# Weight rings without padding, `y` and the mix at byte 64 of a 2048-byte line, and a longer block-wise end in a two-layer fp32 encoder

## The chip, the core and the metric

One core of a Trainium2 chip runs the whole program in one launch. The metric is the time of one execution in microseconds on the device; the kernel before took 2162.01 us (median of 3 runs, 2161.94 to 2162.14). TensorE (PE) multiplies; each of its multiplications is a weight load (PEld, the stationary operand, 128 columns) and a matmul (the moving operand). VectorE (DVE), ScalarE (ACT) and GpSimd (POOL) do the elementwise work, SyncE (SP) issues the transfers.

## What is computed

An encoder of two residual layers on 256 tokens of width 2048, all in fp32. Layer 0 has chunked and differential attention, layer 1 a sparse attention with an indexer and a shared latent. Cut to what matters here:

```python
for layer in range(DEPTH):                       # DEPTH = 2
    h = rmsnorm(x, attn_norm[layer])
    if layer % 2 == 0:
        p = h @ even_w_in[e]                     # 2048 x 6144: q, k, v of both head groups
        mix = jnp.concatenate([oa, ob], axis=-1) @ even_w_out[e]      # 2048 x 2048
    else:
        p = h @ odd_w_in[o]                      # q, latent, index parts
        mix = oc.reshape(b, s, C_Q_W) @ odd_w_out[o]                  # 2048 x 2048
    x = x + mix
    h = rmsnorm(x, ffn_norm[layer])
    x = x + (jax.nn.silu(h @ w_gate[layer]) * (h @ w_up[layer])) @ w_down[layer]   # 2048 x 5632, 5632 x 2048
return rmsnorm(x, final_norm)
```

## The kernel before

**Split numbers.** Every fp32 operand is held as a rounded high part and the rest: `xs` (normalized input), `y` (FFN hidden) and `mix` hold `[tile, 2, 256]` with the high part at index 0 and the low part at index 1, so that the two are 1024 bytes apart and one tile takes 2048 bytes of a partition. A weight piece (128 x 1024 fp32, 512 KB) lands in `wl`, a ring of 5; ACT rounds it to `wh` (line 145), DVE writes the rest to `wo` (line 146). `wh` and `wo` are rings of 3, so the next piece's `wh` can be written once PE is done with the piece three before it. `load_w` does this, `next_w` keeps three pieces ahead.

**Two forms of product.** `gemm_t` has the weights stationary and the activations moving. For each piece it makes 4 groups (`n`) of 4 matmuls, by `products`: two of 512 columns with `wh` (high and low part of an `xs` tile together), then two of 256 columns with `wo` (high part alone). This is the gate and up projection (352 pieces), q and k (64), the odd layer's q (32) and its index part (8): 456 pieces with 1824 groups, whose results are named `acc`. `gemm_n` has the activations stationary and the weights moving, 512 columns at a time. For each piece, two token blocks `b`, two tiles `j` and three matmuls by `mm3`: (`y` high, `wh`), (`y` high, `wo`), (`y` low, `wh`), so 12 matmuls. This is `w_down` (176 pieces), the two output projections (32 each) and the four v projections (32): 272 pieces, whose results are named `nat`. All of them go through `mm`, so that they are recorded at one line, 181.

**The places.** Inside a partition each `wh` and `wo` buffer is padded on both sides by `OFF` = 16 floats, so the ring's step is 4224 bytes and not 4096. The v pieces and `w_uv` are written 64 bytes into the buffer (`moving`, `UVO`), all others at its start. `spacer` tiles of `SP0`, `SP1` and `SPY` floats set where `mix` (layer 0, layer 1) and `y` begin. In the built program the places, as bytes modulo 2048, are:

| | place 0 | place 1 | place 2 |
|---|---|---|---|
| `wh` | 1600 | 1728 | 1856 |
| `wo` | 1984 | 64 | 192 |

`xs` is at 128, `y` at 1088 in both layers, `mix` at 1088 in layer 0 and at 448 in layer 1. The loads go round the ring, so that pieces follow each other in places 1, 0, 2, 1 and so on as seen by PE.

**The end.** The last of the four column groups of `w_down` in layer 1 is made with `last=2`: 20 pieces are worked off with both token blocks alternating, and the last two pieces first for block 0 and then for block 1. After each block `finish_block` adds the residual (line 312, DVE), squares (line 307, ACT), forms 1/rms (lines 271, 255, 257), scales four column parts (lines 674, 676, 678) and writes them out (line 679).

Each engine's instructions stand in the order of the code; nothing reorders them.

Of the kernel before, what the change touches and what calls it, by code (L numbers as in the profile page):

```python
# [25 lines left out]
FT = DFF // P  # L26
# [13 lines left out]
def encoder_kernel(  # L40
# [41 lines left out]
    def bank(shape, name):  # L82
        return psum.tile(shape, F32, name=name, tag="ps")


    OFF = 16
    SP0, SP1, SPY = 16, 16, 96
    UKO, UVO = 0, OFF
    OUT0 = [4, 5, 6, 7, 0, 1, 2, 3]
    QUADS = (2, 3, 0, 1)  # L90

# [10 lines left out]
    def moving(pieces):  # L102
        return ((src, OFF) for src in pieces)

# [25 lines left out]
    def load_w(cuts=1, between=None):  # L130
# [7 lines left out]
        wl = wpool.tile([P, width], F32, name="wl", tag="wl", bufs=5)  # L138
        wh, wo = (wpool.tile([P, width + 2 * OFF], F32R, name=n, tag=n, bufs=3)[:, off:off + width] for n in ("wh", "wo"))
        for i in range(cuts):  # L140
# [8 lines left out]
    def next_w():  # L149
        while len(ahead) < 3:  # L150
            n = len(ahead)
            load_w()
            if len(ahead) == n:
                break
        return ahead.popleft()
# [4 lines left out]
    def pump(n=1):  # L160
        for _ in range(n):
            while steps:
                try:
                    next(steps[0])
                    break
                except StopIteration:
                    steps.popleft()
# [15 lines left out]
    def mm3(out, a, b, start, stop):  # L183
        (ah, al), (bh, bl) = a, b
        mm(out, ah, bh, start, False)
        mm(out, ah, bl, False, False)
        mm(out, al, bh, False, stop)
# [26 lines left out]
    def gemm_n(lhs, nk, order=None, last=0, done=None):  # L214

        banks = [bank([P, 512], f"nat{i}") for i in range(2)]
        order = list(range(nk // 2)) if order is None else order

        def block_products(b, i, w):
            wh, wo = w  # L220
            for j in range(2):
                h, l = lhs(2 * order[i] + j)
                t = slice(b * P, (b + 1) * P)
                c = slice(j * 512, (j + 1) * 512)
                mm3(banks[b], (h[:, t], l[:, t]), (wh[:, c], wo[:, c]),
                    i == 0 and j == 0, i == len(order) - 1 and j == 1)

        for i in range(len(order) - last):
            w = next_w()
            for b in range(2):  # L230
                block_products(b, i, w)
                pump()
        if last:
            ws = [next_w() for _ in range(last)]
            for b in range(2):
                for i, w in enumerate(ws):
                    block_products(b, len(order) - last + i, w)
                done(b, banks[b])
        return banks

    def pairs(act):
        return lambda kt: (act[:, kt, 0, :], act[:, kt, 1, :])
# [59 lines left out]
    def new_sums():  # L302
        return {"sums": small.tile([P, 2, 4], F32, name="sums", tag="sums", bufs=2)}
# [5 lines left out]
    def add_block(bk, b, g, st):  # L309

        c = xn[:, b, 512 * g:512 * g + 512]
        nc.vector.tensor_tensor(out=c, in0=bk, in1=c, op=ALU.add)
        add_squares(st, b, g)
# [15 lines left out]
    def add_residual(banks, g, gi, st):  # L329
        for b in range(2):  # L330
            add_block(banks[b], b, g, st)
        steps.append(transpose_steps(g, gi))
# [284 lines left out]
    def ffn(st):  # L617

        with tc.tile_pool(name="ffn", bufs=1) as fp:
            fp.tile([P, SPY], F32, name="spacer")  # L620
            y = fp.tile([P, FT, 2, S], F32R, name="y")
            for g in range(FT // 4):
                gb = gemm_t(xs, KT)
                if g == 0:
                    drain()
                ga = fp.tile([P, 4, S], F32, name="ga", tag="ga", bufs=1)
                for n in range(4):
                    a = ga[:, n, :]
                    combined(a, gb[n])
                    nc.vector.tensor_tensor(out=a, in0=a, in1=st["rr"], op=ALU.mult)  # L630
                    th = fp.tile([P, S], F32, name="th", tag="th", bufs=3)
                    nc.scalar.activation(th, a, AF.Tanh, scale=0.5)  # L632
                    nc.vector.scalar_tensor_tensor(out=a, in0=th, scalar=1.0, in1=a, op0=ALU.add, op1=ALU.mult)  # L633
                    nc.gpsimd.tensor_tensor(out=a, in0=a, in1=st["rs"], op=ALU.mult)  # L634
                ub = gemm_t(xs, KT)
                for n in range(4):
                    t = 4 * g + n
                    a = ga[:, n, :]
                    u = fp.tile([P, S], F32, name="up", tag="up", bufs=2)
                    combined(u, ub[n])  # L640
                    nc.vector.tensor_tensor(out=a, in0=a, in1=u, op=ALU.mult)
                    split((y[:, t, 0, :], y[:, t, 1, :]), a)
            yield y, fp

    def ffn_layer(st, gi, last):
        out = new_sums()
        body = ffn(st)
        y, fp = next(body)
        if last:
            gf = fp.tile([P, D], F32, name="gf", tag="ga", bufs=1)  # L650
            nc.sync.dma_start(out=gf, in_=bass.AP(tensor=gfin.tensor, offset=gfin.offset, ap=[[0, P], [1, D]]))
        for g in range(4):
            fin = last and g == 3
            banks = gemm_n(pairs(y), FT, last=2 if fin else 0, done=partial(finish_block, out, gf) if fin else None)
            if not last:
                add_residual(banks, g, gi, out)
            elif not fin:
                for b in range(2):
                    add_block(banks[b], b, g, out)
                    c = slice(512 * g, 512 * g + 512)  # L660
                    nc.gpsimd.tensor_tensor(out=xn[:, b, c], in0=xn[:, b, c], in1=gf[:, c], op=ALU.mult)
        for _ in body:
            pass
        return out
# [15 lines left out]

    steps.append(norm_steps(st, "n1", 0.5))
    st = ffn_layer(st, 2, False)


# [9 lines left out]
    banks = [bank([P, 2, S], f"x{n}") for n in range(3)]  # L694
# [135 lines left out]

    steps.append(norm_steps(st, "n3", 0.5))
    ffn_layer(st, 4, True)


# [61 lines left out]
```

## Time and profile before

| | |
|---|---|
| median of 3 runs | 2162.01 us |
| the profiled execution | 2161.7 us, of which its span 2159.9 us |
| PE busy | 2148.4 us, 99% of the span |
| DVE, ACT, POOL busy | 60%, 49%, 8% |
| chain that ended last | PE 98% (`acc` 59%, `nat` 35%) |
| granted TensorE clock | 0.999 of 2.4 GHz |

Matmuls are pipelined: the duration of one in the record is longer than the time from its start to the next one's start. How fast PE goes is read from the distances of starts, or from a stretch's length and its count.

### The profile page before, as it was taken

How to read it: one execution, taken by the hardware profiler on the slowest of the kernel's cores; microseconds unless marked ns; L12 is line 12 of the kernel's file. 1: busy time of each engine (PE TensorE's matmuls, PEld its weight loads, DVE VectorE, ACT ScalarE, POOL GpSimd, SP SyncE). 2: the span in 40 equal slices, each digit the busy share in tenths (PEclk: the TensorE clock that was granted, in tenths of full speed). 3: DMA queues.
4: the chain of work that ended last, by engine and by line, in shares of the span. 5: the costliest groups of instructions: out<-in, count | busy, mean ns of one | idle time of the engine just before them, and what ended most of it. 6: DMA issues, size and time to landing. Idle time of an engine off the chain costs nothing.

```text
span 2159.9 us, 29908 instructions
## 1 busy us (share of the span) xinstructions
PE 2148.4 (99%) x11380; PEld 1836.1 (85%) x11380; DVE 1299.2 (60%) x1882; ACT 1065.6 (49%) x1603; POOL 178.6 (8%) x194
## 2 busy tenths in 40 slices
PE   9999999999999999999999999999999999999998
PEld 8888888888888888888888888888888888888886
DVE  6665555666666666544446977556666666654443
ACT  6554554545454454444435566445454454543443
POOL 0111000000000000000001241000000000000000
PEclk9999999999999999999999999999999999999999
DMA  9565556555555665555656554555555555566564
GB/s 319 174 178 167 175 167 184 184 186 186 189 188 189 187 188 191 186 185 187 193 168 214 166 156 151 182 186 186 189 189 188 187 189 190 186 207 193 187 193 138
DMA packets 114975, 401.95 MB, mean 186 GB/s; under 512 B 12618, under 2 KB 16526, under 8 KB 114702
## 3 DMA queue, kind: packets, MB, share of 16 engines
q1 hardware_dynamic: 114686, 399.90, 58.7%
q8 instruction: 89, 1.46, 0.3%
q14 instruction: 56, 0.46, 0.1%
q10 hardware_dynamic: 144, 0.13, 0.0%
HBM read 397.84 MB, written 2.14 MB: 185 GB/s over the span
## 4 chain that ended last, share of the span: by engine, by line
PE 98%; DMA 1%; DVE 0%; ACT 0%; issue 0%; SPq 0%; ACTq 0%; POOLq 0%; POOL 0%
PE acc L181 59%; PE nat L181 35%; PE x L181 1%; PE uk L181 1%; DMA xt<-in_xT 1%; PE xT L323 0%; PE is L181 0%; PE c3o L181 0%; PE a0o L181 0%; PE a1o L181 0%; PE c2o L181 0%; PE c0o L181 0%; PE c1o L181 0%; DVE wo L146 0%; PE b31o L181 0%
## 5 line engine op out<-in xcount | busy, mean ns | idle before, releaser
L146 DVE TENSOR_TENSOR wo<-wl,wh 128x1024 fp32r<-128x1024 f32 (+2 forms) x747 | 925.9, 1240 | 805.2 <-ACT wh L145 797.3
L145 ACT ACTIVATE wh<-wl 128x1024 fp32r<-128x1024 f32 (+2 forms) x747 | 786.9, 1054 | 910.1 <-PE acc L181 491.9
L181 PE MATMUL acc<-xs,wh 128*128 128x512 f32 x3648 | 1147.7, 396 | 0.5 <-ACT wh L145 0.5
L181 PEld LDWEIGHTS acc<-xs,wo 128*128 128x128 f32 x3648 | 685.6, 188 | 160.2 <-DVE wo L146 1.6
L181 PE MATMUL acc<-xs,wo 128*128 128x256 f32 x3648 | 731.1, 281 | 0.6 <-DVE wo L146 0.5
L181 PEld LDWEIGHTS acc<-xs,wh 128*128 128x128 f32 x3648 | 560.3, 188 | 3.2 <-ACT wh L145 0.8
L181 PE MATMUL nat<-wh,y 128*128 128x512 f32 x1408 | 441.6, 394 | 0.0
L181 PEld LDWEIGHTS nat<-wh,y 128*128 128x128 f32 x1408 | 264.2, 188 | 61.4
L181 PE MATMUL nat<-wo,y 128*128 128x512 f32 x704 | 276.4, 393 | 0.0
L181 PE MATMUL nat<-wh,mix 128*128 128x512 f32 x512 | 166.7, 397 | 0.0
L181 PEld LDWEIGHTS nat<-wo,y 128*128 128x128 f32 x704 | 132.3, 188 | 29.8
L337 ACT ACTIVATE u<-acc 128x256 f32<-128x256 f32 x228 | 86.3, 379 | 61.4 <-PE acc L181 32.3
L181 PEld LDWEIGHTS nat<-wh,mix 128*128 128x128 f32 x512 | 96.1, 188 | 21.1
L181 PE MATMUL nat<-wo,mix 128*128 128x512 f32 x256 | 100.4, 392 | 0.0
L181 PE MATMUL nat<-wh,xs 128*128 128x512 f32 x256 | 83.2, 393 | 0.0
L634 POOL TENSOR_TENSOR ga<-ga,n1rs 128x256 f32<-128x256 f32 x44 | 37.7, 867 | 440.3 <-DVE ga L633 417.2
L634 POOL TENSOR_TENSOR ga<-ga,n3rs 128x256 f32<-128x256 f32 x44 | 36.6, 843 | 441.4 <-DVE ga L633 418.3
L181 PEld LDWEIGHTS nat<-wh,xs 128*128 128x128 f32 x256 | 48.1, 188 | 10.0
L181 PEld LDWEIGHTS nat<-wo,mix 128*128 128x128 f32 x256 | 48.2, 188 | 9.7
L181 PE MATMUL nat<-wo,xs 128*128 128x512 f32 x128 | 50.0, 391 | 0.0
L298 ACT ACTIVATE xs<-xT,gc 128x256 fp32r<-128x256 f32 x48 | 22.4, 467 | 31.0 <-DVE xs L299 31.0
L632 ACT ACTIVATE th<-ga 128x256 f32<-128x256 f32 x88 | 33.8, 410 | 5.8 <-DVE ga L630 5.7
(804 smaller groups left out, 1056.3 us busy)
## 6 DMA issues: line engine op xcount, KB each, us to landing
wl<-in_w_gate SPq DMA_DIRECT2D x176, 512.0 KB, 3.8
wl<-in_w_up SPq DMA_DIRECT2D x176, 512.0 KB, 3.6
wl<-in_w_down SPq DMA_DIRECT2D x176, 512.0 KB, 3.6
wl<-in_w_ein SPq DMA_DIRECT2D x93, 512.0 KB, 3.6
wl<-in_w_eout SPq DMA_DIRECT2D x32, 512.0 KB, 3.6
wl<-in_w_oq SPq DMA_DIRECT2D x32, 512.0 KB, 3.6
wl<-in_w_oout SPq DMA_DIRECT2D x32, 512.0 KB, 3.5
wl<-in_w_oi SPq DMA_DIRECT2D x8, 512.0 KB, 4.2
```

The costliest lines, as they stand in the source:

```text
L145: latest["act"] = nc.scalar.activation(wh[:, c], wl[:, c], AF.Copy)
L146: nc.vector.tensor_tensor(out=wo[:, c], in0=wl[:, c], in1=wh[:, c].bitcast(F32), op=ALU.subtract)
L181: nc.tensor.matmul(out, a, b, start=start, stop=stop, skip_group_check=True)
L298: nc.scalar.activation(xs[:, t, 0, :], src, AF.Copy, scale=g)
L337: nc.scalar.activation(u[:m], b[:m, 0, :], AF.Copy)
L632: nc.scalar.activation(th, a, AF.Tanh, scale=0.5)
L634: nc.gpsimd.tensor_tensor(out=a, in0=a, in1=st["rs"], op=ALU.mult)
```

## The change

`OFF` becomes 0, so the rings of `wh` and `wo` step by 4096 bytes and no piece is written 64 bytes in. The spacers move `y` and `mix`. The last three pieces (before: two) are worked off block by block.

```diff
-    OFF = 16
-    SP0, SP1, SPY = 16, 16, 96
-    UKO, UVO = 0, OFF
+    OFF = 0
+    SP0, SP1, SPY = 464, 112, 32
+    UKO, UVO = 0, 0
@@
-            banks = gemm_n(pairs(y), FT, last=2 if fin else 0, done=partial(finish_block, out, gf) if fin else None)
+            banks = gemm_n(pairs(y), FT, last=3 if fin else 0, done=partial(finish_block, out, gf) if fin else None)
```

In the built program `wh` and `wo` are then at 1600 modulo 2048 in all three places, `y` and both `mix` at 64, `xs` still at 128. Tiles behind the rings move with them. DVE, ACT, POOL and SP have the same instructions in the same order as before. PE has the same matmuls; only those of the last three pieces change places among each other.

On PE, from the point where the two programs part, the kernel before ends the third-last piece (`wh_18924`, `wo_18925`) with block 1 (`nat1`) before it takes up the second-last (`wh_18942`) and the last (`wh_18960`) for block 0 (`nat0`):

```order
L181 MATMUL nat1_18616<-wh_18924,y_12732 128x512
L181 MATMUL nat1_18616<-wo_18925,y_12732 128x512
L181 MATMUL nat1_18616<-wh_18924,y_12732 128x512 x2
L181 MATMUL nat1_18616<-wo_18925,y_12732 128x512
L181 MATMUL nat1_18616<-wh_18924,y_12732 128x512
L181 MATMUL nat0_18615<-wh_18942,y_12732 128x512
L181 MATMUL nat0_18615<-wo_18943,y_12732 128x512
L181 MATMUL nat0_18615<-wh_18942,y_12732 128x512 x2
L181 MATMUL nat0_18615<-wo_18943,y_12732 128x512
L181 MATMUL nat0_18615<-wh_18942,y_12732 128x512
L181 MATMUL nat0_18615<-wh_18960,y_12732 128x512
L181 MATMUL nat0_18615<-wo_18961,y_12732 128x512
```

The block 1 part of piece 18924 (6 matmuls) stands ahead of block 0's last 12 matmuls.

On PE at the same point the changed kernel goes on with block 0:

```order
L181 MATMUL nat0_18615<-wh_18942,y_12732 128x512
L181 MATMUL nat0_18615<-wo_18943,y_12732 128x512
L181 MATMUL nat0_18615<-wh_18942,y_12732 128x512 x2
L181 MATMUL nat0_18615<-wo_18943,y_12732 128x512
L181 MATMUL nat0_18615<-wh_18942,y_12732 128x512
L181 MATMUL nat0_18615<-wh_18960,y_12732 128x512
L181 MATMUL nat0_18615<-wo_18961,y_12732 128x512
L181 MATMUL nat0_18615<-wh_18960,y_12732 128x512 x2
L181 MATMUL nat0_18615<-wo_18961,y_12732 128x512
L181 MATMUL nat0_18615<-wh_18960,y_12732 128x512
L181 MATMUL nat1_18616<-wh_18924,y_12732 128x512
L181 MATMUL nat1_18616<-wo_18925,y_12732 128x512
```

Block 0 is complete 6 matmuls earlier, the last piece is wanted 6 matmuls earlier, and 18 matmuls of block 1 follow in place of 12.

## Rows read from the trace of the kernel before

**Rows 1.** The page: span, busiest engine, granted clock by slice.
```profile
span 2159.9 us, 29908 instructions
...
PE 2148.4 (99%) x11380; PEld 1836.1 (85%) x11380; DVE 1299.2 (60%) x1882; ACT 1065.6 (49%) x1603; POOL 178.6 (8%) x194
...
PEclk9999999999999999999999999999999999999999
```

**Rows 2.** The page, costliest groups: busy us, mean ns, idle before, releaser.
```profile
L181 PE MATMUL acc<-xs,wh 128*128 128x512 f32 x3648 | 1147.7, 396 | 0.5 <-ACT wh L145 0.5
...
L181 PE MATMUL nat<-wh,y 128*128 128x512 f32 x1408 | 441.6, 394 | 0.0
```

**Rows 3.** Chain that ended last, its two longest stretches: start us, us, what.
```profile
410.50 479.55 PE acc L181 x2736
...
1906.77 241.39 PE nat L181 x1044
```

**Rows 4.** Timeline, layer 1, `w_down`: a matmul and the weight load beside it.
```profile
1000.18 0.63 PE L181 MATMUL nat<-wh,y 128*128 128x512 f32 x2
...
1000.41 0.19 PEld L181 LDWEIGHTS nat<-wo,y 128*128 128x128 f32 x1
1000.65 0.40 PE L181 MATMUL nat<-wo,y 128*128 128x512 f32 x1
```

**Rows 5.** Timeline, `acc`: starts of pieces, and second groups of two.
```profile
606.65 0.63 PE L181 MATMUL acc<-xs,wh 128*128 128x512 f32 x2
607.36 0.62 PE L181 MATMUL acc<-xs,wh 128*128 128x512 f32 x2
...
609.44 0.62 PE L181 MATMUL acc<-xs,wh 128*128 128x512 f32 x2
...
612.25 0.63 PE L181 MATMUL acc<-xs,wh 128*128 128x512 f32 x2
612.96 0.63 PE L181 MATMUL acc<-xs,wh 128*128 128x512 f32 x2
...
615.06 0.63 PE L181 MATMUL acc<-xs,wh 128*128 128x512 f32 x2
...
617.85 0.62 PE L181 MATMUL acc<-xs,wh 128*128 128x512 f32 x2
```

**Rows 6.** Timeline, `w_down`: the first `wo` matmul of seven pieces.
```profile
1990.07 0.39 PE L181 MATMUL nat<-wo,y 128*128 128x512 f32 x1
...
1992.83 0.39 PE L181 MATMUL nat<-wo,y 128*128 128x512 f32 x1
...
1995.62 0.40 PE L181 MATMUL nat<-wo,y 128*128 128x512 f32 x1
...
1998.41 0.40 PE L181 MATMUL nat<-wo,y 128*128 128x512 f32 x1
...
2001.18 0.39 PE L181 MATMUL nat<-wo,y 128*128 128x512 f32 x1
...
2003.95 0.39 PE L181 MATMUL nat<-wo,y 128*128 128x512 f32 x1
...
2006.72 0.39 PE L181 MATMUL nat<-wo,y 128*128 128x512 f32 x1
```

**Rows 7.** Timeline of the end: last piece's `wh` and `wo`, the two blocks' finish.
```profile
2142.18 0.62 PE L181 MATMUL nat<-wh,y 128*128 128x512 f32 x2
...
2142.61 1.06 ACT L145 ACTIVATE wh<-wl 128x1024 fp32r<-128x1024 f32 x1 [1.69 <-PE nat L181]
...
2143.70 1.23 DVE L146 TENSOR_TENSOR wo<-wl,wh 128x1024 fp32r<-128x1024 f32 x1 [1.52 <-ACT wh L145]
...
2148.18 0.69 DVE L312 TENSOR_TENSOR xn<-nat,xn 128x512 f32<-128x512 f32 x1 [3.26 <-PE nat L181]
...
2150.53 0.40 PE L181 MATMUL nat<-wh,y 128*128 128x512 f32 x1
...
2151.08 0.75 DVE L674 SCALAR_TENSOR_TENSOR xn<-xn,n40r,gf 128x512 f32<-128x512 f32 x1
...
2151.74 0.69 DVE L312 TENSOR_TENSOR xn<-nat,xn 128x512 f32<-128x512 f32 x1
2152.46 0.63 ACT L307 ACTIVATE sq<-xn 128x512 f32<-128x512 f32 x1 [0.45 <-DVE xn L312]
...
2154.63 0.75 DVE L674 SCALAR_TENSOR_TENSOR xn<-xn,n41r,gf 128x512 f32<-128x512 f32 x1
```

## The prediction, made before the changed kernel ran

> **What bounds the kernel now.** I read the page first. PE is busy 2148.4 of 2159.9 us, and the granted clock is at its upper level (2.4 GHz) in all 40 slices [rows 1]. The two large groups of matmuls have idle times of 0.5 and 0.0 us ahead of them in the whole execution [rows 2], so PE does not wait for weights, for DVE or for ACT. Then the chain: 2736 `acc` matmuls in 479.55 us and 1044 `nat` matmuls in 241.39 us without a break [rows 3]. So the time is the number of matmuls by the distance of their starts, and a change that leaves the number as it is can act in two ways only: on that distance, and on the 9 us behind the last matmul.
>
> The distance: a piece of `gemm_t` has 16 matmuls, so 479.55 / 2736 x 16 = 2.804 us; one of `gemm_n` has 12, so 241.39 / 1044 x 12 = 2.775 us [rows 3]. That is 0.231 us for each `nat` matmul of 512 columns, and 512 columns at one per 2.4 GHz cycle would be 0.213. Something adds 8%. Beside each matmul runs the weight load of the next one, begun when the matmul begins: the second `wh` matmul of the row at 1000.18 and the load for `wo` both start at 1000.41 [rows 4]. Both read the same memory.
>
> Now the view that matters for this change, the starts of single pieces. Which place of the ring a piece has, I took from the built program's addresses. In `gemm_t` the piece in place 1 takes 609.44 - 606.65 = 2.79 us, place 0 takes 612.25 - 609.44 = 2.81, place 2 takes 615.06 - 612.25 = 2.81, and place 1 again 617.85 - 615.06 = 2.79 [rows 5]. In `w_down` the pieces in places 1, 0, 2, 1, 0, 2 take 2.76, 2.79, 2.79, 2.77, 2.77 and 2.77 us [rows 6], and the six of them 16.65. The same instructions on the same amounts, and times that go by the place (and, in `w_down`, by the lap). Addresses therefore count, by about 1%. Nothing else in the profile tells the three places apart.
>
> **The change part by part.** The sum is made against the profiled execution, 2161.7 us (span 2159.9 and 1.8 around it); the median of the runs is 0.3 us above it.
>
> *The rings and the tiles behind them.* No instruction is added or removed. Before, `wh` and `wo` lie 384 bytes apart modulo 2048 in each place, which is 128 modulo 256; after, they lie alike. Towards the activations: `wh` in place 0 begins 1600 - 128 = 1472 behind `xs` and 1600 - 1088 = 512 behind `y`. After, each `wh` and each `wo` is 1472 behind `xs` and 1600 - 64 = 1536 behind `y` and `mix`; 1536 and 512 differ by 1024, the distance of `y`'s high and low part, so for `wh` the new arrangement is the one that place 0 has now. The new `wo` at 1600 has a like in place 1: `wo` at 64 there differs from it by 512, which is the step from one group `n` to the next, so the four groups read the same four residues in another order, and towards `y` it is 1024 behind, again 512 steps. So the nearest rows are place 0 for the `wh` matmuls and place 1 for the `wo` matmuls.
>
> For `gemm_t`, with half of its matmuls from each: (2.81 + 2.79) / 2 = 2.80, against 2.804 now, so -0.004 x 456 pieces = -1.8 us. For `gemm_n`, eight matmuls of twelve with `wh`: place 0 takes 2.78 as a mean of its two laps and place 1 takes 2.765, (2 x 2.78 + 2.765) / 3 = 2.775, the same as now: 0 x 272 pieces.
>
> This is a composition of halves that never ran together, so I bound it from both sides by groups of four matmuls. The fastest stretch: the three groups that follow the first in place 1 take (609.44 - 607.36) / 3 = 0.693 us. All groups so, a piece is 2.773 and `gemm_t` gains 0.031 x 456 = 14.1 us. The slowest: the first group after a change of place takes 607.36 - 606.65 = 0.71 and 612.96 - 612.25 = 0.71 [rows 5]. All groups so, a piece is 2.84 and `gemm_t` loses 0.036 x 456 = 16.4 us. For `gemm_n` the best piece (2.76) and the worst (2.79) give -0.015 x 272 = -4.1 and +0.015 x 272 = +4.1 us [rows 6]. I take the composition and keep both ends for the range.
>
> DVE and ACT read and write the same tiles at other addresses. Their work in a lap is far from filling it (60% and 49% [rows 1]) and PE did not wait for them, so I put their part at 0.
>
> The Trainium skill speaks against any effect of the places. Its page "SBUF — State Buffer", section "Who interferes with whom", says that PE has two independent read ports, one for the moving operand and one for weight loads, and never waits on anyone. Its page "TensorE: Matmul & The Clock Gate", section "Step-by-step: what each phase is for", says that loading the next weights takes no read bandwidth from the running matmul. By these the first part of the change is worth 0 and the sum would hold the end alone. The 2.79 and 2.81 us of the places [rows 5] do not agree with that, and I go by the rows.
>
> *The last three pieces.* Before, the last matmul starts at 2150.53 and is recorded for 0.40, so it ends at 2150.93. DVE's add for block 1 could start some 0.02 later, as it did for block 0. It starts at 2151.74, because DVE is still scaling block 0 (from 2151.08, 0.75 us) [rows 7]. That is 0.79 us on the path to the end. After, block 0 is complete 6 matmuls, 6 x 0.231 = 1.39 us, earlier against the last matmul; its scaling would end at 2151.83 - 1.39 = 2150.44, ahead of 2150.95. All of the 0.79 goes. What comes next is the same chain: squares on ACT, whose block 0 work is over by then as well, the sums, 1/rms, the scaling and the last transfers.
>
> The price of it: the last piece is wanted earlier. PE takes up the third-last piece at about 2142.41 (second matmul of the row at 2142.18), so block 0 reaches the last piece 12 matmuls later, at 2145.19, and its `wo` 0.23 after that. That `wh` is ready at 2142.61 + 1.06 = 2143.67, its `wo` at 2143.70 + 1.23 = 2144.93 [rows 7]. Its buffer comes free when it did before, with the end of the fourth-last piece. So 1.5 and 0.5 us are left and PE doesn't wait; if the cover failed, PE would stand still for what is missing, at most the 1.23 us of the `wo` instruction. So this part is worth -0.8, between -0.8 and +0.4.
>
> *Sum*: -1.8 + 0 - 0.8 = -2.6, and 2161.7 - 2.6 = 2159.1 us, with the 0.3 to the median 2159.4. I say 2159.
>
> **The rivals.** For them, as for the forecast, about 0.2% (4.3 us) is what a measurement of this kernel can tell from no change, so "the same" reaches from 2157.7 to 2166.3.
>
> *All like the fast groups.* With equal places there is no jump from one arrangement to another any more; the first group after each jump is the slow one (0.71), and the groups settle at 0.693 afterwards in place 1. If the new arrangement settles as well as that, the time is 2161.7 - 14.1 - 0.8 = 2146.8 us. For it: the settling is in the rows. Against it: places 0 and 2 settle at 0.70 to 0.71, and half of the new arrangement is place 0's.
>
> *All at odds.* The opposite: now that `wh` and `wo` lie alike, each matmul meets its neighbour's weight load in the same position, and what hurts one hurts all four of a group. The present offset of 128 bytes modulo 256 between `wh` and `wo` may be what spreads it. If every second group is at 0.71 in place of 0.701 (8.2 us of the 16.4) and `gemm_n` runs at its worst piece throughout (4.1), the time is 2161.7 + 8.2 + 4.1 - 0.8 = 2173.2, slower than before. It decides as soon as the mean of the groups goes over 0.703. For it: places 0 and 2, two of the three, are the slow ones now. Against it: place 1's `wo` has the new residues and is part of the fastest piece.
>
> *The places do nothing.* The differences between places would come from the jumps or the lap alone and stay as a mean; then 2161.7 - 0.8 = 2160.9. Against it: three like `w_down` pieces at 2.77 follow three at 2.76 to 2.79 with the addresses repeated, which shows that the lap counts too, but the place with the shortest time stays place 1 in both forms.
>
> **How the numbers follow.** Forecast 0.42, fast groups 0.25, at odds 0.21, no effect 0.12. The forecast's own range is 2154 to 2164, from an error of 0.01 us in a `gemm_t` piece (4.6 us), the resolution of the rows. About a third of it lies below 2157.7 and a little above 2166.3. So faster 0.25 + 0.14 = 0.39; slower 0.21 + 0.02 = 0.23; the same 0.38. The range for 8 in 10 takes in most of the two outer cases: 2146 to 2173.
>
> **What would show it.** Behind the change all `gemm_t` pieces must last alike, with no order of places; 2.80 us for them and 2.775 for `w_down` confirms the composition, 2.77 the first rival, 2.82 or more the second. If they still differ in a pattern of three, the addresses were not the reason. At the end the add for block 1 must start 0.02 us behind the last matmul, with no DVE work ahead of it, and PE must show no wait ahead of the last piece. The prediction is wrong if the mean distance of `acc` or `nat` matmuls moves by more than 0.4%.

## The result, and the profile after

The changed kernel takes 2132.28 us (median of 4 runs, 2131.90 to 2132.77), the kernel before 2161.98 (4 runs, 2161.85 to 2162.14). The ratio is 0.9863 with a 95% interval of 0.9846 to 0.988: 29.7 us faster. That lies 27 us below the predicted 2159 and 14 us below the lower end of its range.

The page of the changed kernel, against [rows 1] (the last line shown is the row of [rows 2]):

```profile
span 2130.5 us, 29908 instructions
...
PE 2119.5 (99%) x11380; PEld 1825.3 (86%) x11380; DVE 1300.6 (61%) x1882; ACT 1067.0 (50%) x1603; POOL 178.4 (8%) x194
...
PEclk9999999999999999999999999999999999999999
...
L181 PE MATMUL acc<-xs,wh 128*128 128x512 f32 x3648 | 1139.3, 393 | 0.1
```

The same instructions, the same clock (granted 0.999 in both), and PE as full as before: what changed is the time from one start to the next. The chain of waits shows it (start us, us, what), against [rows 3]:

```profile
54.37 6.99 PE nat L181 x30
...
330.82 19.09 PE nat L181 x84
...
407.89 471.97 PE acc L181 x2736
...
1067.71 54.45 PE nat L181 x240
...
1333.90 19.09 PE nat L181 x84
...
1882.93 235.32 PE nat L181 x1038
```

The same view of the kernel before, for the short stretches that the prediction did not show:

```profile
54.54 6.90 PE nat L181 x30
...
332.33 19.43 PE nat L181 x84
...
1081.41 55.48 PE nat L181 x240
...
1349.27 19.36 PE nat L181 x84
```

An `acc` piece now takes 471.97 / 2736 x 16 = 2.760 us (2.804 before), a `w_down` piece 235.32 / 1038 x 12 = 2.720 (2.775), an output projection piece 19.09 / 7 = 2.727 (2.776 in layer 0, 2.766 in layer 1), and a v piece, 2.5 of which are the 30 matmuls of the first stretch, 2.80 (2.76). By pieces: `acc` 456 x 0.044 = -20.2 us, `w_down` 176 x 0.054 = -9.5, the projections 32 x (0.049 + 0.039) = -2.8, v 32 x 0.036 = +1.2, the end -0.8: together -32.1. The span fell by 29.4, so 2.7 were given back. 0.4 of it is there at the first long `acc` stretch (it starts at 17.26 in place of 16.88). About 1.5 lie in layer 1's attention: from the end of layer 0's `w_down` (1136.89 before, 1122.16 after) to the first long stretch of the output projection (1349.27 and 1333.90) the time fell by 0.6 us, from 212.38 to 211.74, where the sum counts 2.2 (40 `acc` pieces and some 10 of the projection). PE's matmuls there stand between short ones of the attention. The view of PE's waits, which listed none there before, lists one after (us in total, times, longest):

```profile
PE c00s L181 <- POOL qs L178: 0.3, 1, 0.3
```

Why the rest of that gain did not come, and where the last 0.8 us are, is not traced to rows.

Single pieces in the timeline (start us, us, engine, line, operation), `gemm_t` at the place of [rows 5] and `w_down` at that of [rows 6]:

```profile
606.45 0.62 PE L181 MATMUL acc<-xs,wh 128*128 128x512 f32 x2
...
609.21 0.62 PE L181 MATMUL acc<-xs,wh 128*128 128x512 f32 x2
...
611.97 0.62 PE L181 MATMUL acc<-xs,wh 128*128 128x512 f32 x2
...
614.73 0.62 PE L181 MATMUL acc<-xs,wh 128*128 128x512 f32 x2
...
1983.65 0.39 PE L181 MATMUL nat<-wo,y 128*128 128x512 f32 x1
...
1986.37 0.39 PE L181 MATMUL nat<-wo,y 128*128 128x512 f32 x1
...
1989.09 0.39 PE L181 MATMUL nat<-wo,y 128*128 128x512 f32 x1
```

Sixteen `acc` matmuls take 2.76, 2.76 and 2.76 us, twelve `nat` matmuls 2.72 and 2.72. The pattern of three is gone.

The end, against [rows 7]:

```profile
2121.16 0.74 DVE L674 SCALAR_TENSOR_TENSOR xn<-xn,n40r,gf 128x512 f32<-128x512 f32 x1
...
2121.92 0.39 PE L181 MATMUL nat<-wh,y 128*128 128x512 f32 x1
2122.35 0.69 DVE L312 TENSOR_TENSOR xn<-nat,xn 128x512 f32<-128x512 f32 x1 [0.44 <-PE nat L181]
...
2125.24 0.75 DVE L674 SCALAR_TENSOR_TENSOR xn<-xn,n41r,gf 128x512 f32<-128x512 f32 x1
```

The last matmul ends at 2122.31 and block 1's add starts 0.04 later; block 0's scaling is over at 2121.90. PE's rows run through without a gap up to there.

### The profile page after: what moved, and what is told of

The parts are those of the page before. It is cut to its first block, busy times and chain, and to the rows that moved or that the text cites. A ratio compares the mean times of both kernels' runs of the same rounds, so it can differ in the third digit from the quotient of the medians.

```text
span 2130.5 us, 29908 instructions
## 1 busy us (share of the span) xinstructions
PE 2119.5 (99%) x11380; PEld 1825.3 (86%) x11380; DVE 1300.6 (61%) x1882; ACT 1067.0 (50%) x1603; POOL 178.4 (8%) x194
## 4 chain that ended last, share of the span: by engine, by line
PE 96%; DVE 2%; ACT 1%; issue 1%; DMA 1%; POOL 0%; SPq 0%; ACTq 0%; POOLq 0%; DVEq 0%
PE acc L181 57%; PE nat L181 34%; PE x L181 1%; DVE wo L146 1%; DMA xt<-in_xT 1%; PE xT L323 0%; PE uk L181 0%; DVE sc L770 0%; DVE sc L780 0%; POOL tm L789 0%; ACT wh L145 0%; DVE m L779 0%; PE c3o L181 0%; PE a1o L181 0%; PE a0o L181 0%
## 5 line engine op out<-in xcount | busy, mean ns | idle before, releaser
L181 PE MATMUL acc<-xs,wo 128*128 128x256 f32 x3648 | 722.8, 279 | 0.9 <-DVE wo L146 0.9
L181 PEld LDWEIGHTS acc<-xs,wh 128*128 128x128 f32 x3648 | 554.7, 188 | 3.1 <-ACT wh L145 0.8
L181 PE MATMUL nat<-wh,y 128*128 128x512 f32 x1408 | 435.6, 390 | 0.0
L181 PEld LDWEIGHTS nat<-wo,y 128*128 128x128 f32 x704 | 132.2, 188 | 27.3
```

The costliest lines, as they stand in the source:

```text
L181: nc.tensor.matmul(out, a, b, start=start, stop=stop, skip_group_check=True)
```

## The experiments

In what follows *distance* is the address of the stationary operand in its partition, in bytes, less that of the moving one, modulo 256. In `acc` the weights are stationary, in `nat` the activations. Where a piece has two distances, that of `wh` stands first; such a piece is called a mixture. All rows of this section are from the chain of waits, unless it says otherwise; L182 to L185 are line 181, moved down by added lines. The table gathers what the runs gave; the pieces are worked out from the long stretches as above (`nat` from `w_down`).

| run | distance in acc | acc piece | distance in nat | nat piece | time |
|---|---|---|---|---|---|
| before | 192/64, 64/192, 192/64 by place | 2.804 | 0/128, 128/0, 0/128 by place | 2.775 | 2162.0 |
| changed kernel | 192 | 2.760 | 0 | 2.720 | 2132.3 |
| rings_only | 192 | 2.760 | 0 | 2.720 | 2134.9 |
| places_only | as before | 2.804 | as before | 2.775 | 2162.3 |
| last3_only | as before | 2.804 | as before | 2.775 | 2161.2 |
| all_plus64 | 0 | 2.787 | 0 | 2.720 | 2141.5 |
| rings_plus128 | 64 | 2.773 | 128 | 2.789 | 2151.9 |
| rings_plus192 | 128 | 2.787 | 64 | 2.800 | 2161.6 (one run) |
| jump_only | 192, 64, 192 by place | 2.764 | 0, 128, 0 by place | 2.749 | 2139.8 |
| wo_plus128 | 192/64 | 2.773 | 0/128 | 2.773 | 2151.6 |
| mixed_swap | 64/192 | 2.773 | 128/0 | 2.747 | 2142.9 |
| wo_plus64 | 192/0 | 2.793 | 0/192 | 2.784 | 2160.5 |
| wo_plus192 | 192/128 | 2.813 | 0/64 | 2.747 | 2159.6 (one run) |
| v_plus64 | 192 | 2.760 | 0 | 2.720 | 2130.7 |

**Which part of the change.** First the parts alone. The rings without padding, all else where it was (against the changed kernel):

```diff
-    SP0, SP1, SPY = 464, 112, 32
+    SP0, SP1, SPY = 208, 208, 288
-    last=3 if fin
+    last=2 if fin
```

> The rings step by 4096 bytes and no piece is written 64 bytes in, as in the changed kernel; y and the mix stay at 1088, 1088 and 448 modulo 2048, and the end is worked off with two pieces as before. Theory 1 (the distance of stationary and moving address modulo 256 counts, and that it is the same for every matmul): acc pieces 2.76 us and y pieces 2.72 us as in the changed kernel, because 1088 and 64 are alike modulo 256 against the rings; only the mix of layer 1 at 448 stands at another distance (128) and may differ; 0.8 us more for the end: 2132 to 2136 us. Theory 2 (the move of y and the mix gave the gain of the nat matmuls): acc 2.76, nat as before at 2.775: 2132.3 + 0.8 + 240 x 0.0545 = 2146 us.

```profile
407.77 471.97 PE acc L181 x2736
...
1357.19 19.59 PE nat L181 x84
1884.42 236.68 PE nat L181 x1044
```

2134.89 us, ratio 0.9875 (0.986 to 0.989): 27.3 of the 29.7 us. `y` at 1088 and at 64 give the same 2.720. Only layer 1's mix, whose 448 stands at distance 128, takes 19.59 / 7 = 2.80 a piece, 2.3 us more on 32 pieces.

Then `y` and the mix alone (against the kernel before):

```diff
-    SP0, SP1, SPY = 16, 16, 96
+    SP0, SP1, SPY = 272, 432, 352
```

> Only y and both mix move to 64 modulo 2048; the padded rings and the end with two pieces stay as before. Theory 1: the distances modulo 256 in acc are untouched (2.804) and in nat still 0 and 128 in turn, as before (2.775); 2160 to 2163 us. Theory 2: nat pieces at 2.72, so 2162 - 13 = 2149 us.

```profile
410.67 479.55 PE acc L181 x2736
...
1907.25 241.39 PE nat L181 x1044
```

2162.28 us, ratio 1.0002 (0.9992 to 1.0011): both long stretches last what they did before to 0.01 us. Theory 2 is out: moving `y` and mix gives no gain by itself.

And the end alone:

```diff
-    last=2 if fin
+    last=3 if fin
```

> The kernel before with the last three pieces worked off by block in place of two; rings, y and mix untouched. The step of the prediction: the add for block 1 starts 0.02 to 0.05 us behind the last matmul in place of 0.8, no wait ahead of the last piece, span and time 0.8 us shorter (2161.2 against 2162.0). Rival: the last piece's wo comes too late when it is wanted 6 matmuls earlier, PE waits up to 1.2 us ahead of it, and the time is the same or 0.4 us longer.

The timeline of its end:

```profile
2150.58 0.40 PE L181 MATMUL nat<-wh,y 128*128 128x512 f32 x1
2151.01 0.69 DVE L312 TENSOR_TENSOR xn<-nat,xn 128x512 f32<-128x512 f32 x1 [0.54 <-PE nat L181]
```

The add starts 0.03 us behind the last matmul's end (0.81 before), the span is 2159.2 (2159.9). The runs' ratio, 0.9996 (0.9987 to 1.0006), can't show 0.8 us by itself; the medians are 2161.18 and 2162.01.

**Whether the distance counts, and which.** Rings, `y` and mix all 64 bytes further on (a spacer ahead of the rings):

```diff
+    const.tile([P, 16], F32, name="shift")
```

> The changed kernel with the rings, y and the mix all 64 bytes further on (rings at 1664, y and mix at 128, xs still at 128 modulo 2048), so that stationary and moving address are alike modulo 256 in all three forms: acc goes from distance 192 to 0, v from 64 to 0, nat on y and mix stays at 0. Theory 1a (which distance it is counts, and 0 is the best): v pieces from 2.80 to 2.72 (32 x 0.08 = -2.6 us) and acc pieces from 2.76 towards 2.72 (456 x 0.04 = -18 us): 2111 to 2130 us, the lower end if acc reaches 2.72. Theory 1b (only that all distances are the same counts, not which): v and acc as in the changed kernel, 2132 us.

```profile
55.11 6.81 PE nat L182 x30
...
407.62 476.52 PE acc L182 x2736
...
1892.24 235.31 PE nat L182 x1038
```

2141.49 us, ratio 0.9905 (0.9888 to 0.9921). `y` and rings moved together and `w_down` stayed at 2.720; `xs` did not move, and both products with it changed: v to 6.81 / 2.5 = 2.72, as expected, and `acc` to 2.787, against what I expected. So in `nat` distance counts, not the address, and 0 is its best value so far. For `acc` it is not: 2.787 here is worse than 2.760. Since `xs` stood at 128 in every run, the runs do not separate, for `acc`, its distance from the ring's own address.

The rings alone moved on, by 128 and by 192 bytes, `y` and mix held at 64:

```diff
+    const.tile([P, 32], F32, name="shift")     # 48 in the other
-    SP0, SP1, SPY = 464, 112, 32
+    SP0, SP1, SPY = 432, 80, 512               # 416, 64, 496
```

> The changed kernel with the rings 128 bytes further on (1728 modulo 2048 in all places), xs, y and mix where they are. Distances, stationary less moving address modulo 256: acc from 192 to 64, nat on y and mix from 0 to 128, v from 64 to 192. From the runs so far acc is 2.760 at 192 and 2.787 at 0, nat 2.72 at 0 and 2.80 at 128 (layer 1's mix in the run with only the rings changed). Theory 1a (the distance itself sets the pitch): nat on y and mix 2.80 throughout, so + 240 x 0.08 = 19 us; acc at 64 not yet seen, 2.76 to 2.80, so 0 to 18 us: 2151 to 2170 us. Theory 4 (the ring's own address counts, not its distance): acc and nat keep 2.76 and 2.72 or move alike in both; no reason for nat to go to just 2.80.

```profile
409.03 474.25 PE acc L182 x2736
...
1896.28 241.22 PE nat L182 x1038
```

> The changed kernel with the rings 192 bytes further on (1792 modulo 2048): acc at distance 128, nat on y and mix at 64, v at 128. Theory 1a: nat on y and mix 2.80, as v was at 64; v 2.80, as layer 1's mix was at 128; acc not yet seen at 128, 2.76 to 2.80: 2151 to 2170 us. Theory 4: as for the ring that lies 128 further on.

```profile
411.49 476.56 PE acc L182 x2736
...
1905.23 242.21 PE nat L182 x1038
```

2151.92 us (ratio 0.9955, 0.9938 to 0.9971) and 2161.62 (one run). Moving only the rings takes `nat` from 2.720 to 2.789 and 2.800, near the 2.80 that the mix at 128 and v at 64 had shown; theory 4 is out for `nat`. For `acc` the four distances 0, 64, 128, 192 give 2.787, 2.773, 2.787, 2.760; for `nat` 0, 64, 128 give 2.720, 2.800, 2.789, and v at 192 (rings_plus128) 2.748. Equal rings by themselves are thus no gain: at 192 bytes further on the kernel with equal places is as slow as the one before.

**Jump or mixture.** Before, two things were unequal: `wh` and `wo` within a piece, and one place and the next. First the jump alone, `wh` and `wo` alike in each place (in this run and the next four other spacers hold `y` and mix at 64):

```diff
-        wh, wo = (wpool.tile([P, width + 2 * OFF], ...)[:, off:off + width] for n in ("wh", "wo"))
+        wh = wpool.tile([P, width + 32], F32R, name="wh", tag="wh", bufs=3)[:, :width]
+        if not latest:
+            wpool.tile([P, 32], F32, name="gap")
+        wo = wpool.tile([P, width + 32], F32R, name="wo", tag="wo", bufs=3)[:, :width]
```

> The changed kernel with the ring's step of 4224 bytes back, but wh and wo alike modulo 256 in each place (wh 1600, 1728, 1856 and wo 64, 192, 320 modulo 2048); y and mix at 64. Within a piece all distances are equal, from piece to piece they jump: acc 192, 64, 192; nat on y and mix 0, 128, 0. From the runs with equal places acc is 2.760 at 192 and 2.773 at 64, nat 2.720 at 0 and 2.789 at 128. Theory 1 additive (each piece takes what its own distance takes): acc (2 x 2.760 + 2.773) / 3 = 2.764, nat (2 x 2.720 + 2.789) / 3 = 2.743, so 2132.3 + 456 x 0.004 + 240 x 0.023 = 2140 us. Theory 6 (the jump itself costs: before, acc is at 2.804 although its two distances, steady in one piece, give 2.773, so 0.031 a piece): acc 2.795, so 14 us more, about 2154 us.

```profile
408.01 472.72 PE acc L184 x2736
...
1887.76 237.82 PE nat L184 x1038
```

2139.78 us, ratio 0.9897 (0.9882 to 0.9911); 2140 was worked out from the distances' own values. `acc` is at 2.764, as the sum says. A jump between pieces that are equal in themselves costs nothing in `acc`, and theory 6 is out; in `nat` it may cost 0.006 a piece (2.749, where the sum says 2.743).

Then the mixture alone, as places 0 and 2 had it, steady over the places (a gap between the two rings):

```diff
-        wh, wo = (wpool.tile([P, width + 2 * OFF], ...)[:, off:off + width] for n in ("wh", "wo"))
+        wh = wpool.tile([P, width], F32R, name="wh", tag="wh", bufs=3)
+        if not latest:
+            wpool.tile([P, 32], F32, name="gap")
+        wo = wpool.tile([P, width], F32R, name="wo", tag="wo", bufs=3)
```

> The changed kernel with the wo ring 128 bytes further on (1728 modulo 2048 in all three places; wh at 1600, y and mix at 64, xs at 128). All places of a ring are alike, so nothing jumps from piece to piece, but wh and wo stand at two distances within each piece (192 and 64 in acc; 0 and 128 in nat), the two that the kernel before has. Theory 1 (a change of distance from matmul to matmul costs): acc and nat pieces go back to about 2.80 and 2.775, 2132 + 20 + 13 = about 2165 us. Theory 3 (only the jump from one place of the ring to the next cost, each piece's own arrangement is free): 2.76 and 2.72 stay, 2132 us.

```profile
410.82 474.24 PE acc L184 x2736
...
952.51 58.24 PE nat L184 x252
...
1014.42 58.81 PE nat L184 x252
...
1897.85 239.90 PE nat L184 x1038
```

2151.59 us, ratio 0.9952 (0.9937 to 0.9967). `nat` loses what was expected and is at 2.773, `acc` loses only 0.013 of the 0.044 a piece. Neither theory gave that number. The two `x252` stretches are the same instructions at the same distances and differ by 1%: a mixture can settle in more than one rhythm.

And as place 1 had it, steady, by the same edit and a shift of both rings:

```diff
+    const.tile([P, 32], F32, name="shift")
```

> The changed kernel with the wh ring at 1728 and the wo ring at 1856 modulo 2048 in all three places (xs 128, y and mix 64): acc wh at distance 64 and wo at 192, nat on y and mix wh at 128 and wo at 0. This is place 1 of the kernel before made steady; the run with wo 128 further on was places 0 and 2 made steady (acc 2.773, nat 2.773 with stretches of 2.80). Theory 8 (the mean over the places is all there is to the kernel before): acc here must be 3 x 2.804 - 2 x 2.773 = 2.866, so 2132.3 + 456 x 0.106 + about 13 = 2194 us. Theory 9 (wh and wo at two distances cost a little, and a change of this arrangement from piece to piece costs more, 0.03 us a piece): acc here 2.77 to 2.79, 2145 to 2160 us.

```profile
408.76 474.25 PE acc L185 x2736
...
1891.22 237.61 PE nat L185 x1038
```

2142.89 us, ratio 0.9911 (0.9894 to 0.9927), 2 us under what theory 9 allowed because `nat` is at 2.747. `acc` is at 2.773 again, so the kernel before is not the mean of its places (2.773 each, 2.804 together), and theory 8 is out. That leaves a two-by-two for `acc`: equal and steady 2.760, equal with jumps 2.764, mixed and steady 2.773, mixed with jumps 2.804. Theory 9 gave the right size: of the 0.044 some 0.013 is the mixture, and by difference 0.031 is left to what only the kernel before has (and the runs that leave its rings alone), a mixture that differs from place to place. That it is paid at the change is not shown. In [rows 5] the piece from 612.25 to 615.06 (place 2) follows one of place 0 with the same distances, 192/64, and is as slow, 2.81; over layer 1's long stretch the means of places 1, 0 and 2 are 2.79, 2.81 and 2.81. The same distances, when all places have them, take 2.773. Either a slower rhythm outlasts the change, or it matters that `wh` and `wo` lay 384 bytes apart before and lie 128 apart in the steady runs; no run separates the two. In `nat` the mixtures themselves (2.773 and 2.747) make up most of the 0.054, and the change of them 0.01 (2.775 against (2 x 2.773 + 2.747) / 3 = 2.764), less than the 0.027 between the two `x252` stretches.

Two other mixtures, the `wo` ring 64 and 192 bytes further on than `wh`, by the edit of wo_plus128 with another gap:

```diff
-            wpool.tile([P, 32], F32, name="gap")
+            wpool.tile([P, 16], F32, name="gap")     # 48 in the other
```

> The changed kernel with the wo ring 64 bytes further on in all places: wh at distance 192 and wo at 0 in acc; wh at 0 and wo at 192 in nat on y and mix. Theory 1 additive: acc the mean of 2.760 and 2.787, 2.773; nat two thirds of 2.720 and one third of 2.748 (v at 192), 2.73; 2132.3 + 456 x 0.013 + 240 x 0.01 = 2141 us. Theory 7 (a matmul and the load that follows it belong together, so mixed distances have a value of their own): anything from 2.74 to 2.81 for acc.

```profile
411.89 477.66 PE acc L184 x2736
...
1905.57 240.82 PE nat L184 x1038
```

> The changed kernel with the wo ring 192 bytes further on in all places: acc wh at 192, wo at 128; nat on y and mix wh at 0, wo at 64. Theory 1 additive: acc 2.773, nat (2 x 2.720 + 2.800) / 3 = 2.747, 2132.3 + 6 + 6.4 = 2145 us. Theory 7: values of their own.

```profile
410.20 481.08 PE acc L184 x2736
...
1907.55 237.60 PE nat L184 x1038
```

2160.50 us (ratio 0.9992, 0.9982 to 1.0002) and 2159.61 (one run). `nat` with 0/64 is at 2.747, as the sum of thirds says; the other three values are not sums: `nat` with 0/192 is at 2.784 where 2.73 was worked out, `acc` at 2.793 and 2.813 where both halves say 2.773. Halves do not add, which is theory 7.

**Which pair it is.** Whether a matmul suffers from the distance to its own stationary operand or to the one that is loaded beside it (layer 0's spacer, `SP0`, is 208 here):

```diff
-    mix = mixp.tile([P, KT, 2, S], F32R, name="mix", tag="mix")
+    mix = mixp.tile([P, KT, 2, S + 32], F32R, name="mix", tag="mix")[:, :, :, :S]
```

> The changed kernel with 128 bytes behind each high and each low part of layer 0's mix (step 2304 bytes, a multiple of 256), so the low part stands 128 bytes further on modulo 256 than the high part; everything else as it was. Only layer 0's output projection (32 pieces) is touched. Of the three matmuls high x wh, high x wo, low x wh: if the distance of a matmul's own two operands counts, the third is at 128; if that of the moving operand and the stationary operand loaded beside it counts, the second is. Either way the 84 matmuls of the long stretches go from 19.09 to between 19.3 and 19.6 us (pieces 2.75 to 2.80); the time goes up 1 to 2.6 us.

The timeline of layer 0's projection:

```profile
340.33 0.40 PE L181 MATMUL nat<-wo,mix 128*128 128x512 f32 x1
...
340.56 0.62 PE L181 MATMUL nat<-wh,mix 128*128 128x512 f32 x2
340.80 0.19 PEld L181 LDWEIGHTS nat<-wo,mix 128*128 128x128 f32 x1
341.02 0.40 PE L181 MATMUL nat<-wo,mix 128*128 128x512 f32 x1
```

From high x `wo` (340.33) it is 0.23 us to low x `wh` (340.56), 0.24 to the next high x `wh` (340.80, where the load of the row begins) and 0.22 to the next. The hundredths of these rows are too coarse, but the means over the two long stretches tell more: high x `wh` 0.227 (0.227 in the changed kernel), high x `wo`, beside which the low part is loaded, 0.233 (0.227), and low x `wh`, which uses it, 0.234 (0.227). Both of the last two are longer, so this does not separate the two. The long stretch is at 19.43, as expected, and the time 2133.70 (one run).

**A version that beats both.** v at distance 0, without a change for `acc`:

```diff
-    OFF = 0
-    SP0, SP1, SPY = 464, 112, 32
-    UKO, UVO = 0, 0
+    OFF = 16
+    SP0, SP1, SPY = 80, 240, 160
+    UKO, UVO = 0, OFF
-        ... wpool.tile([P, width + 2 * OFF], ...
+        ... wpool.tile([P, width + 4 * OFF], ...
```

> The changed kernel with 256 bytes of padding behind each wh and wo buffer (places 1600, 1856, 64 and 320, 576, 832 modulo 2048, all alike modulo 256) and with the v pieces and w_uv written 64 bytes into the buffer; y and mix at 64, xs at 128. Theory 1a with 256 as the modulus: acc stays 2.760, y and mix 2.72, and v goes from 2.80 to 2.72: 32 x 0.08 = 2.6 us less than the changed kernel, 2129.5 to 2130 us, a ratio of 0.985 to before. Theory 5 (the places of a ring must be equal modulo 2048, or the step must be a power of two): acc and nat go back to 2.79 to 2.80 and 2.77: about 2160 us.

```profile
54.47 6.82 PE nat L181 x30
...
406.49 471.97 PE acc L181 x2736
...
1881.40 235.32 PE nat L181 x1038
```

2130.67 us (2130.55 to 2130.82), ratio 0.9856 (0.9841 to 0.9871); the highest of its runs is 1.1 us below the lowest of the changed kernel's. v is at 6.82 / 2.5 = 2.73. That is 32 x 0.07 = 2.2 us, of which 1.6 arrive. And three places that differ modulo 2048 but not modulo 256 behave as one place: theory 5 is out, padding as such was never the harm.

## Why the prediction was wrong

By the sign that it set itself the prediction is wrong: the mean time between starts fell by 1.6% in `acc` and by 2.0% in `nat`, and it allowed 0.4%.

*What bounds the kernel*: right. The time between starts and the end moved; the clock and PE's share stayed, and PE's waits on other engines are 2.6 us in the whole execution (1.9 before).

*Addresses count*: right, and larger than read. The prediction took 1% from [rows 5, 6] as the size of the effect. Those rows only compare three places that are all unequal in themselves. The range over the runs is 2.760 to 2.813 for `acc` and 2.720 to 2.800 for `nat`. The rule cited from the Trainium skill (the page "SBUF — State Buffer", section "Who interferes with whom": PE has two independent read ports and never waits on anyone), read as the prediction did, that places are worth nothing, does not agree: 64 bytes of shift take `acc` from 2.760 to 2.787.

*The composition*: this is the step that failed. "So the nearest rows are place 0 for the `wh` matmuls and place 1 for the `wo` matmuls" gave -1.8 us and 0; measured -20.2 and -11.1 (w_down, projections and v together). It assumed that each half of a piece keeps its own time whatever the other half does. The runs with `wo` 64 and 192 bytes on show that halves do not add. Place 0's `wh` and place 1's `wo` both stand at distance 192 from `xs`; they were read off pieces of 2.81 and 2.79 us, and with all matmuls at 192 a piece takes 2.760. Of the 0.044 us that `acc` gained, 0.013 is the mixture within a piece and 0.031 is left, by difference, to mixtures that differ from place to place, in a way that stays open; in `nat` the mixtures by themselves make up most of the 0.054. No single row of before can show this, since every row of it is in that state.

*The bounds*: wrong for the same reason. "The fastest stretch" of 0.693 us a group was the best of the mixed state (a steady mixture runs at 2.773 / 4 = 0.693). The mean group is now 2.760 / 4 = 0.690, and `w_down` at 2.720 lies far below its "best" piece of 2.76. Both bounds together gave -18, short of the -31 that came.

*The rivals*: "All like the fast groups" had the right sign and part of the reason. It blamed the jump; in `acc` jumps between equal pieces are free (2.764), and the loss comes with the mixtures. It also had no gain for `gemm_n`, which gave about 11 us. "All at odds" feared that equal `wh` and `wo` hurt all four of a group at once. At this distance they don't; with the rings 192 bytes further on `nat` would have been at 2.800, above its worst piece of before (2.79), and the time at 2161.6 us, no slower than before. "The places do nothing" is out: the pattern of three is gone and 20 us of `acc` with it.

*The v pieces* got no term of their own: they stand in the 272 `nat` pieces, though with `xs` and not `y` or mix on the other side. They became slower, 1.2 us, the only form that lost.

*The end*: right, 0.8 us, in the changed kernel and in the run with this edit alone.

## What to carry to other kernels

Where PE is full and every matmul brings a weight load, as here, work out, for each form of product, the distance of stationary and moving address modulo 256 and make it one number for all matmuls of the form; then try the four multiples of 64, since equality alone can be as slow as before (2161.6 us). A row of a mixed state bounds only mixed states: for an arrangement that never ran, the range has to be wider than the best and worst rows seen. Where a kernel has several forms against the same operand, give each its own offset, as the v pieces got here.

## What the runs showed of the hardware

The time from one matmul of 512 columns to the next, with a weight load beside it, was 2.720 / 12 = 0.227 us at distance 0 and 2.800 / 12 = 0.233 at 64, at a granted clock of 0.999 in both. Shifts of 1024 bytes (`y` at 1088 and 64, both 2.720) and of 256 (the rings of the last run, 471.97 and 235.32 us as in the changed kernel) changed nothing. `acc`, with two matmuls of 512 and two of 256 columns in turn, was fastest at 192 (2.760). With the low part alone at 128, the matmul beside its load and the one that uses it both went from 0.227 to 0.233 and 0.234. Why these values, and whether it is the load beside a matmul or its own operands, stays open.
